# New prices for scans, row sums, transpositions and scaled additions in the engine model that orders a mixer layer's work

## The chip, the cores and the metric

One core of one Trainium2 chip runs the whole layer. The metric is the device time of one execution in microseconds (us), the median of several runs. The engines are TensorE (PE, matrix products, with its weight loads shown as PEld), VectorE (DVE), ScalarE (ACT), GpSimd (POOL) and SyncE (SP, which here only starts transfers). Each works through a list of its own in order, and they wait for each other by semaphores.

## The reference: what is computed

A layer on 256 tokens of width 2048, in float32: a SwiGLU block, a token mixer, a second SwiGLU block, each added to its input, and a last norm.

```python
x = x + 0.5 * swiglu(rms_norm(x, ffn1_norm), w_gate, w_up, w_down)      # inner width 5632
proj = rms_norm(x, mix_norm) @ w_in
y = concat(rwkv7_mix(proj[..., :3360]), hgrn2_mix(proj[..., 3360:]))    # 16 heads x 64, 8 heads x 128
x = x + y @ w_out
x = x + 0.5 * swiglu(rms_norm(x, ffn2_norm), w_gate2, w_up2, w_down2)
return rms_norm(x, final_norm)
```

The mixer has two recurrences over the tokens. `rwkv7_mix` is a delta rule with a decay for each channel; `hgrn2_mix` is a gated linear recurrence. Both are computed here in blocks of tokens.

## The kernel before

**Weights.** Nearly all of PE's time goes into products with weights. They come from memory in pieces of 128x1024 float32 (`raw`), one after the other in the order of the list `pieces`. To keep float32's accuracy, a piece is split in two: ACT rounds it to a shorter form (`hi<-raw`), and DVE or POOL subtracts that from the piece (`lo<-raw,hi`). PE multiplies with hi on all 256 tokens in two levels (512 columns) and with lo on the upper level alone (256 columns), so a piece is 8 + 8 matmuls. There are four buffers for raw, hi and lo each. When piece i is used up, `split_to(i + 5)` puts the split of a later piece on ACT's and DVE's or POOL's lists, about three pieces ahead of its use. In the first eight pieces and the last four lo always goes to DVE. In the others `spare` chooses: it goes to POOL if the model says that DVE would be done with it over 1500 ns later than POOL while mixer work is pending, or later at all while none is.

**The mixer's work.** The mixer's products with weights (jobs k, r, v for rwkv, and f, q, i, g for hgrn, in two halves 0 and 1 of the heads) stand in one loop (`for i, kk, part in order()`). Everything else of the mixer runs beside them, in generators: `rwkv(half)` and `hgrn(half)`. After every matmul of the loop `poll` gives the first two pending generators a step if `max(V.until, S.until)`, the model's time at which DVE's and ACT's lists are done, is at most 2500 ns behind the model's time of PE. Inside a generator `need(tile)` puts the rest off until the model says that the tile is ready.

**The model.** V, S and G wrap the three engines (class `Engine`). Each call of an operation goes through `call` in `__getattr__`: it asks `cost` for the operation's time, a fixed part and a rate for each element of a partition, moves the engine's `until` on by it and notes in `model.ready` when the output will be there. `Products` does the same for PE, whose time `model.pe` is the model's now. No number of the model reaches the chip; it only decides in which order instructions are written and which engine takes a lo. A scheduler then keeps that order by and large when it fills each engine's list.

**Names in the mixer.** In the rwkv half, k's section scales with `tensor_scalar` on POOL, takes reciprocals and `scalar_tensor_tensor` products on DVE, 128x256 at a time and four for a half, then 128x1024 products on POOL (`t<-t,t`) and DVE, then running products over tokens (`tensor_tensor_scan`, 128x260, four for each call, which the order of the program prints as SCALAR_TENSOR_TENSOR b8<-b8,cst), and products into the operands `b8`. Then follows a chain of 62 dependent small products on DVE, for which `state["chain"]` is set, so that lo stays on DVE. The hgrn half works in levels s = 0 to 7: for each DVE makes a product `t<-t,tot` and POOL one `q<-q,tot`, and PE multiplies the two (`ps<-q,t`).

Of the kernel before, what the change touches and what calls it, by code (L numbers as in the profile page):

```python
# [97 lines left out]
def names_of(xs):  # L98
    return [getattr(getattr(x, "tensor", x), "name", None) for x in xs if hasattr(x, "shape")]
# [21 lines left out]
class Engine:  # L121
# [3 lines left out]
    def cost(self, op, n):  # L125
        rate = self.model.RATE[self.name]
        if op == "reciprocal":
            rate *= 6
        elif self.name == "vector" and op in ("tensor_copy", "tensor_scalar"):
            rate *= 0.6  # L130
        elif self.name == "gpsimd" and op == "memset":
            rate *= 0.2
        elif op == "dma_start":
            return 1000.0
        return self.model.FIXED[self.name] + rate * n
# [4 lines left out]
    def __getattr__(self, op):  # L140
        fn = getattr(self.engine, op)

        def call(*args, **kwargs):
            m = self.model
            cost = self.cost(op, math.prod(args[0].shape[1:]))
            begin = max(self.until, m.now())
            self.until = begin + cost
            done = max(begin, m.wait(*args)) + cost + m.LATENCY + (5000.0 if op == "dma_start" else 0.0)
            for n in names_of(args[:1]):
                m.ready[n] = done  # L150
            return fn(*args, **kwargs)  # L151

        return call
# [1217 lines left out]
```

## Time and profile before

| | |
|---|---|
| time, median of 3 runs | 2063.84 us (2062.35 to 2064.65) |
| the profiled execution | 2062.84 us, of which the span is 2061.1 |
| PE busy | 2017.2 us, 98% of the span |
| DVE busy | 1377.9 us, 67% |
| ACT busy | 1006.0 us, 49% |
| POOL busy | 390.2 us, 19% |
| mean granted clock of PE | 0.99 of full speed |
| lo's made by DVE (128x1024) | 605, mean 1350 ns |
| lo's made by POOL (128x1024) | 70, mean 2617 ns |

The profile counts an engine as busy from the start to the end of its instructions. A matmul's end is modelled, so the place to look at is where PE does not have a next matmul to start. An idle time in the timelines stands in brackets with what ended it: [3.65 <-POOL lo L151] means that the engine stood still for 3.65 us until POOL's lo was there. L151 is the line of the helper through which every operation of DVE, ACT and POOL goes, and L171 and L175 are those of PE. Buffer numbers are left out of the names in the trace.

### The profile page before, as it was taken

How to read it: one execution, taken by the hardware profiler on the slowest of the kernel's cores; microseconds unless marked ns; L12 is line 12 of the kernel's file. 1: busy time of each engine (PE TensorE's matmuls, PEld its weight loads, DVE VectorE, ACT ScalarE, POOL GpSimd, SP SyncE). 2: the span in 40 equal slices, each digit the busy share in tenths (PEclk: the TensorE clock that was granted, in tenths of full speed). 3: DMA queues.
4: the chain of work that ended last, by engine and by line, in shares of the span. 5: the costliest groups of instructions: out<-in, count | busy, mean ns of one | idle time of the engine just before them, and what ended most of it. 6: DMA issues, size and time to landing. Idle time of an engine off the chain costs nothing.

```text
span 2061.1 us, 31577 instructions
## 1 busy us (share of the span) xinstructions
PE 2017.2 (98%) x12766; PEld 1762.0 (85%) x12766; DVE 1377.9 (67%) x1498; ACT 1006.0 (49%) x1199; POOL 390.2 (19%) x220
## 2 busy tenths in 40 slices
PE   8999999999999999899989899999999999999998
PEld 7888888888888888788868788888888888888887
DVE  7665565555565688986888668856565655555657
ACT  6444444444444466465556545544444344434434
POOL 1221110111011032322343104222111011101101
PEclk9999999999999999999999999999999999999999
DMA  7655665556556565443434435555656555655653
GB/s 252 202 183 191 194 191 187 188 185 194 190 184 194 185 233 174 155 138 124 131 115 149 150 105 182 190 189 183 194 187 191 189 187 189 195 191 184 194 187 120
DMA packets 106146, 368.33 MB, mean 179 GB/s; under 512 B 11632, under 2 KB 18032, under 8 KB 105744
## 3 DMA queue, kind: packets, MB, share of 16 engines
q1 hardware_dynamic: 104352, 359.97, 54.0%
q0 software_dynamic: 1104, 6.06, 0.8%
q8 instruction: 100, 1.64, 0.3%
q14 instruction: 46, 0.38, 0.1%
q10 hardware_dynamic: 544, 0.28, 0.0%
HBM read 362.08 MB, written 4.19 MB: 178 GB/s over the span
## 4 chain that ended last, share of the span: by engine, by line
PE 50%; DVE 2%; POOL 1%; issue 0%; ACT 0%; DVEq 0%; POOLq 0%; ACTq 0%
PE mm L171 46%; PE ps L171 4%; DVE t L151 1%; POOL t L151 1%; DVE lo L151 1%; ACT t L151 0%; DVE xts L151 0%; DVE b L151 0%; POOL lo L151 0%; PE ps L175 0%; POOL b L151 0%; ACT hi L151 0%; DVEq L1367 0%; ACT inv L151 0%; ACT itok L151 0%
## 5 line engine op out<-in xcount | busy, mean ns | idle before, releaser
L171 PE MATMUL mm<-t,hi 128*128 128x512 f32 x5264 | 1287.0, 393 | 4.8 <-DVE t L151 4.3
L171 PEld LDWEIGHTS mm<-t,hi 128*128 128x128 f32 x5264 | 961.6, 189 | 189.1 <-ACT hi L151 3.9
L151 DVE TENSOR_TENSOR lo<-raw,hi 128x1024 fp32r<-128x1024 f32 (+1 forms) x615 | 818.6, 1335 | 403.2 <-ACT hi L151 379.7
L151 ACT CAST hi<-raw 128x1024 fp32r<-128x1024 f32 (+1 forms) x685 | 712.8, 1042 | 685.1 <-PE mm L171 426.9
L171 PEld LDWEIGHTS mm<-t,lo 128*128 128x128 f32 x5296 | 695.3, 191 | 52.8 <-POOL lo L151 11.4
L171 PE MATMUL mm<-t,lo 128*128 128x256 f32 x5296 | 712.0, 284 | 13.8 <-POOL lo L151 10.5
L151 POOL TENSOR_TENSOR lo<-raw,hi 128x1024 fp32r<-128x1024 f32 x70 | 183.2, 2617 | 548.3 <-ACT hi L151 529.7
L151 POOL TENSOR_TENSOR t<-t,inv 128x1024 f32<-128x1024 f32 x22 | 69.0, 3134 | 730.2 <-ACT t L151 730.2
L151 DVE TENSOR_TENSOR t<-mm,t 128x512 f32<-128x512 f32 x122 | 83.7, 686 | 171.1 <-ACT t L151 171.1
L151 ACT COPY t<-mm 128x512 f32<-128x512 f32 x122 | 71.4, 585 | 241.2 <-PE mm L171 225.9
L151 DVE TENSOR_TENSOR t<-t,t 128x512 fp32r<-128x512 f32 (+25 forms) x243 | 124.5, 516 | 13.9 <-ACT t L151 7.6
L151 DVE SCALAR_TENSOR_TENSOR xts<-mm,xts 128x512 f32<-128x512 f32 x126 | 86.6, 687 | 28.0 <-PE mm L171 27.6
L151 ACT CAST t<-t 128x512 fp32r<-128x512 f32 x72 | 43.7, 616 | 13.1 <-DVE t L151 4.9
L151 DVE TENSOR_TENSOR t<-t,inv 128x1024 f32<-128x1024 f32 (+1 forms) x35 | 42.5, 1215 | 1.0
L151 DVE RECIPROCAL t<-t 128x256 f32<-128x256 f32 x24 | 41.4, 1736 | 2.4 <-ACT t L151 2.3
L151 POOL TENSOR_TENSOR t<-t,t 128x1024 f32<-128x1024 f32 (+1 forms) x9 | 25.4, 2820 | 73.3 <-ACT hi L151 45.0
L151 DVE SCALAR_TENSOR_TENSOR t<-xts,vec,t 128x256 fp32r<-128x256 f32 x48 | 28.6, 616 | 12.5 <-ACT t L151 12.4
L151 ACT ACTIVATE t<-t 128x1024 f32<-128x1024 f32 (+2 forms) x32 | 32.7, 1023 | 4.5 <-DVE t L151 4.4
L151 ACT COPY t<-ps 32x512 f32<-32x512 f32 (+8 forms) x44 | 19.7, 448 | 27.4 <-PE ps L171 26.4
L151 ACT ACTIVATE t<-xts,vec 128x256 fp32r<-128x256 f32 x48 | 23.0, 504 | 19.5 <-DVE xts L151 18.3
L171 PE MATMUL mm<-hi,t 128*128 128x512 f32 x128 | 32.4, 392 | 0.0
L151 POOL TENSOR_TENSOR t<-t 128x1020 f32<-128x1020 f32 (+1 forms) x7 | 17.5, 2506 | 65.9 <-DVE t L151 48.0
(134 smaller groups left out, 723.0 us busy)
## 6 DMA issues: line engine op xcount, KB each, us to landing
raw<-in_ffn_w_up_dram SPq DMA_DIRECT2D x176, 512.0 KB, 3.9
raw<-in_ffn_w_down_dram SPq DMA_DIRECT2D x176, 512.0 KB, 3.4
raw<-in_ffn_w_gate_dram SPq DMA_DIRECT2D x173, 512.0 KB, 3.9
raw<-in_w_in_dram SPq DMA_DIRECT2D x96, 512.0 KB, 3.3
raw<-in_w_out_dram SPq DMA_DIRECT2D x32, 512.0 KB, 3.3
raw<-in_w_i_dram SPq DMA_DIRECT2D x16, 512.0 KB, 3.3
raw<-in_w_lora_dram SPq DMA_DIRECT2D x6, 512.0 KB, 3.4
spill<-xts POOLq DMA_DIRECT2D x1, 2048.0 KB, 10.8
```

The lines of the kernel that those rows point to most:

```text
L151: return fn(*args, **kwargs)
L171: return self.engine.matmul(out, a, b, **kwargs)
```

## The change

The method that prices an operation gets three more cases: a row sum or a scan counts twice the rate, a transposition on DVE 1.5 times, a `scalar_tensor_tensor` on DVE of up to 256 elements 1.8 times. And a row sum is counted by the elements that it reads (`args[1]`) and no longer by those that it writes. The rest of the file is the same; its lines are numbered 6 higher.

```diff
@@ -126,6 +126,12 @@
         rate = self.model.RATE[self.name]
         if op == "reciprocal":
             rate *= 6
+        elif op in ("tensor_reduce", "tensor_tensor_scan"):
+            rate *= 2
+        elif self.name == "vector" and op == "transpose":
+            rate *= 1.5
+        elif self.name == "vector" and op == "scalar_tensor_tensor" and n <= 256:
+            rate *= 1.8
         elif self.name == "vector" and op in ("tensor_copy", "tensor_scalar"):
             rate *= 0.6
         elif self.name == "gpsimd" and op == "memset":
@@ -142,7 +148,7 @@
 
         def call(*args, **kwargs):
             m = self.model
-            cost = self.cost(op, math.prod(args[0].shape[1:]))
+            cost = self.cost(op, math.prod(args[op == "tensor_reduce"].shape[1:]))
             begin = max(self.until, m.now())
             self.until = begin + cost
             done = max(begin, m.wait(*args)) + cost + m.LATENCY + (5000.0 if op == "dma_start" else 0.0)
```

By DVE's fixed 90 ns and 1.04 ns for an element the model's prices go from 356 to 569 ns for a 128x256 `scalar_tensor_tensor`, from 360 to 631 for a scan of 260, from 356 to 2220 for a row sum of 128x1024 to 128x256, from 1155 to 1687 for a 128x1024 transposition.

All engines together do the same operations as before, but for one more load of an activation table on ACT, and 14 lo's (128x1024) are made by POOL that DVE made before: one at the start, five at the end of the first FFN, three more between the mixer's start and the end of the second rwkv half's k section, five behind that. Many operations of DVE, ACT and POOL change places in the mixer. The three places below are those that the prediction speaks of.

The first is POOL's list in the k section of the first rwkv half: scalings t<-t,vec of 128x256, products t<-t,t of 128x1024, and lo's. Before:

```order
L151 TENSOR_SCALAR t4_6876<-t4_6877,vec_92 128x256
L151 TENSOR_TENSOR lo_7142<-raw_7034,hi_7141 128x1024
L151 TENSOR_SCALAR t4_6876<-t4_6877,vec_92 128x256 x2
L151 TENSOR_TENSOR t4_6877<-t4_6877,t4_7074 128x1024
L151 TENSOR_SCALAR t4_6876<-t4_6840,vec_92 128x256 x4
L151 TENSOR_TENSOR t4_6876<-t4_6876,t4_7082 128x1024
L151 TENSOR_TENSOR lo_7195<-raw_7114,hi_7194 128x1024
L151 TENSOR_TENSOR b8_7396<-t4_7082,b8_7235 128x16x64
```

After:

```order
L157 TENSOR_SCALAR t4_6890<-t4_6891,vec_92 128x256 x3
L157 TENSOR_TENSOR lo_7192<-raw_7090,hi_7191 128x1024
L157 TENSOR_SCALAR t4_6890<-t4_6891,vec_92 128x256
L157 TENSOR_TENSOR t4_6891<-t4_6891,t4_7124 128x1024
L157 TENSOR_SCALAR t4_6890<-t4_6840,vec_92 128x256 x4
L157 TENSOR_TENSOR t4_6890<-t4_6890,t4_7058 128x1024
L157 TENSOR_TENSOR b8_7424<-t4_7058,b8_7253 128x16x64
L157 TENSOR_TENSOR t4_7296<-t4_7186 128x4x255
L157 TENSOR_TENSOR lo_7407<-raw_7327,hi_7406 128x1024
```

No lo stands right behind both 128x1024 products any more, where lo_7195 did; one (lo_7192) stands ahead of them, between the third and the fourth scaling, and the next (lo_7407) behind the whole section.

The second is POOL's list at the same section of the second rwkv half. Before:

```order
L151 TENSOR_TENSOR t4_8998<-t4_8998,t4_9235 128x1024
L151 TENSOR_SCALAR t4_8997<-t4_8677,vec_92 128x256 x4
L151 TENSOR_TENSOR t4_8997<-t4_8997,t4_9065 128x1024
L151 TENSOR_TENSOR lo_9354<-raw_9245,hi_9353 128x1024
L151 TENSOR_TENSOR t4_9320<-t4_9167 128x4x255
L151 TENSOR_TENSOR b8_9604<-t4_9065,b8_9440 128x16x64
```

After:

```order
L157 TENSOR_TENSOR t4_9268<-t4_9155 128x4x255
L157 TENSOR_SCALAR t4_9127<-t4_9128,vec_92 128x256 x4
L157 TENSOR_TENSOR t4_9128<-t4_9128,t4_9359 128x1024
L157 TENSOR_SCALAR t4_9127<-t4_8604,vec_92 128x256 x4
L157 TENSOR_TENSOR lo_9423<-raw_9299,hi_9422 128x1024
L157 TENSOR_TENSOR t4_9127<-t4_9127,t4_9031 128x1024
L157 TENSOR_TENSOR b8_9650<-t4_9031,b8_9488 128x16x64
L157 TENSOR_TENSOR lo_9535<-raw_9446,hi_9534 128x1024
```

The lo in the group (lo_9354 before, lo_9423 after, of other weights) now stands ahead of the second 128x1024 product, the product t<-t of 128x4x255 has gone from behind the group to ahead of it, and one more lo (lo_9535) stands behind the product into b8.

The third is DVE's list at the chain of 62 small products (t2) of the second rwkv half, into which lo's and the levels' products t4<-t4,tot are mixed. Before, its end:

```order
L151 TENSOR_TENSOR t2_9946<-t2_9946,t2_9947 128x2x15
L151 TENSOR_TENSOR lo_10297<-raw_10168,hi_10296 128x1024
L151 TENSOR_TENSOR t2_9947<-t4_9944,t2_9946 128x16
L151 TENSOR_TENSOR t4_10223<-t4_10122,tot0_10124 128x64x8
L151 TENSOR_TENSOR t2_9946<-t2_9946,t2_9947 128x16
L151 TENSOR_TENSOR t4_10344<-t4_10223,tot1_10225 128x32x16
```

After, its beginning:

```order
L157 STREAM_TRANSPOSE t4_10084<-t4_10029 128x1024
L157 TENSOR_TENSOR lo_10108<-raw_9900,hi_10107 128x1024
L157 TENSOR_TENSOR t2_10087<-t4_10084,t2_10086 128x31
L157 TENSOR_TENSOR t4_10175<-t4_10073,tot0_10075 128x64x8
L157 TENSOR_TENSOR t2_10086<-t2_10086,t2_10087 128x31
```

And after, its end:

```order
L157 TENSOR_TENSOR t2_10086<-t2_10086,t2_10087 128x2x15
L157 TENSOR_TENSOR t2_10087<-t4_10084,t2_10086 128x16
L157 TENSOR_TENSOR t4_10302<-t4_10175,tot1_10177 128x32x16
L157 TENSOR_TENSOR lo_10475<-raw_10362,hi_10474 128x1024
L157 TENSOR_TENSOR t4_10355<-mm_10201,t4_10355 128x512
L157 TENSOR_TENSOR t2_10086<-t2_10086,t2_10087 128x16
```

The 64x8 product moves from the chain's end to right behind its first link, and the next level's, 32x16, takes the place at the end.

## Rows read from the trace of the kernel before

**Rows 1.** Table by stage: stretch and length, each engine's busy us, clock, DMA.

```profile
core 0: us, PE busy (x) PEld busy (x) DVE busy (x) ACT busy (x) POOL busy (x), PEclk, DMA share, GB/s
42.00:820.00 778.00, 778.00 (x4475) 686.67 (x4474) 492.34 (x471) 367.29 (x409) 125.28 (x51) 1.00 0.59 192
820.00:1275.00 455.00, 426.18 (x3610) 358.19 (x3609) 364.95 (x496) 256.37 (x349) 139.26 (x108) 0.98 0.42 136
1275.00:2048.00 773.00, 773.00 (x4474) 684.09 (x4473) 481.67 (x474) 351.73 (x390) 115.64 (x42) 1.00 0.58 185
...
800.00:850.00 50.00, 46.26 (x259) 39.70 (x258) 48.42 (x43) 31.18 (x37) 24.07 (x14) 0.97 0.40 130
```

**Rows 2.** PE's timeline: start, us, what, count, in brackets idle before and releaser.

```profile
838.12 2.08 PE L171 MATMUL mm<-t,lo 128*128 128x256 f32 x8 [3.65 <-POOL lo L151]
...
861.78 1.10 PE L171 MATMUL ps<-t,bones_r 128*128 128x512 f32 x3 [0.74 <-DVE t L151]
...
1048.00 1.21 PE L171 MATMUL mm<-t,lo 128*128 128x256 f32 x8 [1.38 <-DVE lo L151]
...
1057.91 2.07 PE L171 MATMUL mm<-t,lo 128*128 128x256 f32 x8 [6.86 <-POOL lo L151]
...
1069.98 1.21 PE L171 MATMUL mm<-t,lo 128*128 128x256 f32 x8 [1.02 <-DVE lo L151]
...
1145.00 1.08 PE L171 MATMUL ps<-q,t 128*32 128x32 f32 x64 [6.80 <-DVE t L151]
```

**Rows 3.** The table by stage again, right behind each long wait.

```profile
838.00:841.30 3.30, 3.17 (x12) 2.89 (x13) 3.30 (x2) 0.00 (x0) 3.22 (x2) 0.50 0.44 159
...
1058.00:1063.20 5.20, 5.20 (x17) 4.43 (x18) 1.31 (x4) 0.00 (x0) 3.85 (x2) 0.50 0.59 202
...
1145.00:1148.50 3.50, 3.50 (x72) 3.15 (x73) 3.50 (x5) 2.33 (x6) 3.34 (x6) 0.50 0.46 149
```

**Rows 4.** POOL's timeline at the first rwkv half's k section.

```profile
825.68 3.44 POOL L151 TENSOR_TENSOR t<-t,t 128x1024 f32<-128x1024 f32 x1
...
835.34 2.73 POOL L151 TENSOR_TENSOR lo<-raw,hi 128x1024 fp32r<-128x1024 f32 x1
```

**Rows 5.** DVE's timeline at the same place.

```profile
825.63 1.22 DVE L151 SCALAR_TENSOR_TENSOR t<-t,t 128x1024 f32<-128x1024 f32 x1 [0.84 <-POOL t L151]
826.77 3.43 DVE L151 TENSOR_TENSOR lo<-raw,hi 128x1024 fp32r<-128x1024 f32 x1
...
830.73 5.21 DVE L151 TENSOR_TENSOR_SCAN b<-b,cst 128x260 f32<-128x260 f32 x4
835.97 3.18 DVE L151 SCALAR_TENSOR_TENSOR b<-t,b 128x1024 f32<-128x1024 f32 x1
...
843.44 2.46 DVE L151 TENSOR_TENSOR_SCAN b<-b,cst 128x260 f32<-128x260 f32 x4
```

**Rows 6.** POOL's timeline at the second rwkv half's k section.

```profile
1042.85 0.48 POOL L151 TENSOR_SCALAR t<-t,vec 128x256 f32<-128x256 f32 x1 [1.65 <-DVE t L151]
1043.42 3.44 POOL L151 TENSOR_TENSOR t<-t,t 128x1024 f32<-128x1024 f32 x1
1046.86 5.04 POOL L151 TENSOR_SCALAR t<-t,vec 128x256 f32<-128x256 f32 x4
...
1054.54 3.31 POOL L151 TENSOR_TENSOR lo<-raw,hi 128x1024 fp32r<-128x1024 f32 x1
```

**Rows 7.** DVE's timeline at the second rwkv half's chain of small products.

```profile
1113.42 0.21 DVE L151 TENSOR_TENSOR t<-t,t 128x31 f32<-128x31 f32 x1
...
1119.87 1.21 DVE L151 TENSOR_TENSOR lo<-raw,hi 128x1024 fp32r<-128x1024 f32 x1
...
1144.16 0.69 DVE L151 TENSOR_TENSOR t<-t,tot 128x512 f32<-128x512 f32 x1
```

**Rows 8.** Timelines of POOL and DVE near the first FFN's end.

```profile
709.95 2.41 POOL L151 TENSOR_TENSOR lo<-raw,hi 128x1024 fp32r<-128x1024 f32 x1 [69.28 <-ACT hi L151]
...
710.81 1.83 DVE L151 SCALAR_TENSOR_TENSOR t<-xts,vec,t 128x256 fp32r<-128x256 f32 x1 [0.58 <-ACT t L151]
...
713.70 0.47 DVE L151 SCALAR_TENSOR_TENSOR t<-xts,vec,t 128x256 fp32r<-128x256 f32 x1
```

## The prediction, made before the changed kernel ran

> **What bounds the kernel now.** I read four views in this order. First the table by stage: outside the mixer TensorE (PE) never stands still, 778.00 of 778 us in the stretch from 42 to 820 us and 773.00 of 773 after 1275 us, and between 820 and 1275 us it is busy 426.18 of 455 us [rows 1]. So all that a new order can win lies in those 455 us: 455 − 426.18 = 28.8 us of standing still. Work cannot be won anywhere else, since the change alters no PE instruction. Second, PE's own timeline of the mixer, for where the 28.8 us stand. Three places hold most of it. Place A: 3.65 us for a lo that POOL makes, then small waits, of which one of 0.74 us is shown and two more of 0.54 and 0.56 us lie beside it. Place B: 1.38, 6.86 and 1.02 us for lo's, the longest again for one made on POOL. Place C: 6.80 us for a product that DVE makes [rows 2]. Together 21.5 us; the other 7.3 us are a dozen waits of 0.2 to 1.5 us. Third, the granted clock: in the stretch right behind the beginning of each long wait it is 0.50, that is the 1.2 GHz level, and PE works 3.17, 5.20 and 3.50 us at it [rows 3]. At half speed half of that is lost: 1.6, 2.6 and 1.8 us, 6.0 in all. The ceiling of any reordering is therefore 28.8 + 6.0 = 34.8 us, 1.7% of the time. Fourth, the timelines of POOL and DVE at the three places, which show what stood ahead of the late tile.
>
> **Place A (first rwkv half, around 820 to 866 us).** Before, POOL takes a 128x1024 product of 3.44 us at 825.68, four scalings and a second product, and only then the lo (lo_7195), at 835.34, which ends at 838.07; PE starts at 838.12 [rows 2, 4]. PE wanted it at 838.12 − 3.65 = 834.47. After, the one lo on POOL at this place (lo_7192) stands ahead of that group, between the third and the fourth scaling, and the second lo of POOL (lo_7407) stands behind the whole group. POOL is at that point of its list at about 825.7 us, when the group begins [rows 4]; a lo takes 2.73 us there [rows 4], and even with 3 us of being held up it is done by 831.4. The long wait goes, with its half clock: −3.65 − 1.6 = −5.25. What is late next: the fourth scaling now waits for that lo, and DVE's product of k (1.22 us at 825.63, after 0.84 us of waiting for POOL [rows 5]) waits for the scaling, so it begins 2.7 to 6.4 us later, at 828.3 to 832.0. Behind it DVE has three lo's (3.43 us for one beside a POOL product, 1.2 for the other two), the four scans (2.46 us without POOL beside them, 5.21 with it), the product into b (3.18 us beside POOL, 1.2 at the least, as the k product of the same size) and lo_7303 (1.2 to 3.43), with 1.1 us for the k product and 0.6 for one more [rows 5]. The sum runs from 12.4 to 19.4 us, so lo_7303 is there between 840.7 and 851.4. PE wants it four pieces of weights after 834.47. A piece is 16 matmuls, by the stretch without a wait 778.00 / 4475 x 16 = 2.78 us [rows 1], so at 845.6. The new wait is 0 to 5.8 us; I take the middle, 2.9, and with it half of the old clock loss, 0.8. A: −5.25 + 2.9 + 0.8 = about −1.6, between −5.3 and +2.1.
>
> **Place B (second rwkv half, around 1040 to 1070 us).** Before, POOL's group of product, four scalings, product, lo begins at 1043.42 and its lo ends at 1054.54 + 3.31 = 1057.85: 14.4 us [rows 6]. PE wanted it at 1057.91 − 6.86 = 1051.05 [rows 2], so the group began 7.6 us ahead of the need. After, the second product stands behind the lo. It takes 1054.54 − (1046.86 + 5.04) = 2.6 us, so the group down to the lo is 11.8 us; and since the scans that ran on DVE beside the scalings come later now, the 5.04 us of scalings may shrink, down to 4 x 0.48 = 1.9 us by the one that stands alone at 1042.85 [rows 6]: 8.7 to 11.8. But the group also begins later against the need. In the order of the program 69 matmuls stand between the first product and the first use of the lo before, 54 after; 15 matmuls at 2.78 us for 16 are 2.6 us. So the group has 5.0 us, and the wait is 3.7 to 6.8; I take 5.2. The two waits beside it, 1.38 and 1.02 us, I put at half, 1.2 together, since neither lo keeps its neighbours, and the clock at 2.2. B: (5.2 + 1.2 + 2.2) − (9.26 + 2.6) = −3.3, between −6 and +1.
>
> **Place C (chain of 62 small DVE products beside the hgrn levels, 1107 to 1150 us).** Before, DVE's chain begins at 1113.42 and the product that PE waits for begins at 1144.16, behind 61 of the 62 links, nine lo's of 1.21 us and three other kinds [rows 7]. After, the 64x8 product stands behind the chain's first link and the next one, 32x16, takes the place at its end: one product less of 0.69 us, or 0.6 from start to start, on DVE; one lo and one predicated copy stand ahead of the chain instead of in it, which leaves the end where it was. PE has 1.0 us more of matmuls between the last score product and the waiting one (32.0 against 30.9 us, each at the pace that the trace shows). So the wait is 6.80 − 0.6 − 1.0 = 5.2, and half of the clock loss behind it that hangs on its length, 0.4, goes too. C: −2.0, between −4 and +1.
>
> **The rest.** Of the 14 lo's that go from DVE to POOL, one lies at the start and five at the end of the first FFN, where PE does not stand still with eight of them on POOL already [rows 1]; they cost nothing; the cover is DVE's slack there, and without it each could cost the 1.4 us worked out next. Three more than before lie between 820 and 1060 us of the mixer, the others behind it. What a lo on POOL does to DVE is in the trace: from 709.95 to 712.36 POOL makes one, and DVE's 128x256 product that begins at 710.81 takes 1.83 us, against 0.47 for the same product a little later [rows 8]. So a moved lo saves DVE its 1.2 us and can cost it 1.4. For three of them up to 4.1 us on DVE, where it is busy 48.42 of 50 us [rows 1]; a third of it, 1.3, reaches PE by my choice, since only stretch A is that full. The first chain starts some 5 us of matmuls later against the hgrn levels beside it, whose waits are among the small ones; I put 0.5 us for that. The earlier row sums at the start and one more activation table on ACT (busy 256 of 455 us [rows 1]) I put at nothing; bounds ±1. The rest: +1.8, between −4 and +5 (the small waits are 7.3 us in all, and one more wait like that of A would be 5).
>
> The Trainium skill, "SBUF — State Buffer", section "Who interferes with whom", says that a DVE instruction with two inputs in SBUF and a GpSimd instruction that reads SBUF exclude each other for the whole instruction, so that the second waits until the first is done. The trace agrees here: the stretched product ends at 712.64, 0.28 us behind POOL's lo. If by that rule the whole 4.1 us reached PE, the rest would be +4.6 and the sum −2.3 instead of −5.1.
>
> **Sum.** −1.6 − 3.3 − 2.0 + 1.8 = −5.1 us. The profiled execution took 2062.84 us (span 2061.1 and 1.7 around it), so its like would take 2057.7. The median of the runs is 1.0 us above it, 2063.84, and against that the forecast is 2058.7 us.
>
> **Rivals.**
> 1. The waits only change place. For it: DVE is full at A [rows 1], no work is taken away, and A's new wait and B's old one are ranges that reach to what is there now. The new prices also stay wrong where the trace has the widest spread: a scan is 0.6 us alone and 1.3 beside POOL [rows 5], and one price cannot be both. Against it: the lo's at A and B do stand nearer the head of POOL's list. Time: 2063.8, give or take 3. The Trainium skill, "Perfetto Trace Analysis", section "Optimizing Scalar/DVE Operations", warns that moving work between GpSimd and DVE may not help because they share a read port; by that rule this is the outcome, and the stretched product [rows 8] speaks for it.
> 2. Slower, by one mechanism: at B a second lo (lo_9535) stands on POOL behind the product into b, which waits for the scans that DVE now makes later, behind three lo's. If DVE is as late there as it was before, that lo comes as late as the first. A second wait like the old one costs 6.86 + 2.6 = 9.5 us; the sum becomes +4.4, 2068.2. It decides for slower from a loss of 5.1 us on. Against it: between the place where it is queued and its first use PE has 9.0 us of matmuls.
> 3. Both waits for POOL go almost wholly: A at its lower end (−5.3), B without the scans beside the scalings (−6), C at −4, and the rest at +1: −14.3, 2049.5. For it speaks that the scans, which stretch POOL's scalings, no longer run beside them at B; against it that DVE must still feed all three places.
>
> **How the numbers follow.** Forecast (gain of 2 to 9 us): 0.45. Rival 1: 0.25. Rival 2: 0.20. Rival 3: 0.10. A measurement of this kernel can tell about 0.2%, 4.1 us, from no change. Faster by more than that: 0.7 of the forecast, all of rival 3, a tenth of rival 1: 0.44. Slower by more: nearly all of rival 2 and a seventh of rival 1: 0.23. Within it: 0.33. The range runs from rival 3's time to rival 2's, 2050 to 2068.
>
> **What would show it.** Right at A: no wait of over 3 us for POOL around 834 us, and a smaller one, for DVE's lo, some four pieces later. Right at B: one wait of 4 to 7 us for a POOL lo, and no second one behind it; a second one is rival 2. Right at C: a wait of about 5 us for DVE's product, at the end of the chain. If the mixer's stretch loses as much as before, 28 us, with the waits elsewhere, rival 1 is it. Wrong altogether would be a wait outside the 455 us, or a changed number of PE's instructions.

## The result, and the profile after

The changed kernel takes 2083.67 us (median, 2082.48 to 2085.62) against 2063.71 of the kernel before on the same chip: a ratio of 1.0098, 95% interval 1.0087 to 1.0110. It is 20 us slower. The forecast was 2058.7, and the range ended at 2068.

The table by stage of the changed kernel (columns as in [rows 1]), its profiled execution having a span of 2083.8 us:

```profile
0.00:42.00 42.00, 35.16 (x177) 29.32 (x178) 31.80 (x44) 26.95 (x43) 8.24 (x15) 0.96 0.78 266
42.00:820.00 778.00, 777.21 (x4465) 685.58 (x4465) 486.81 (x462) 362.30 (x401) 133.42 (x55) 1.00 0.59 192
820.00:1275.00 455.00, 424.60 (x3567) 357.96 (x3564) 355.98 (x479) 257.70 (x353) 145.43 (x111) 0.96 0.40 133
1275.00:1345.00 70.00, 60.84 (x337) 52.20 (x336) 56.17 (x63) 32.30 (x43) 32.66 (x14) 0.95 0.45 153
1345.00:2048.00 703.00, 703.00 (x4043) 621.21 (x4042) 422.36 (x389) 311.15 (x332) 98.77 (x35) 1.00 0.59 189
```

Two of these stretches in the kernel before:

```profile
0.00:42.00 42.00, 36.32 (x186) 29.77 (x187) 33.29 (x46) 27.85 (x44) 5.46 (x14) 1.00 0.80 274
1275.00:1345.00 70.00, 70.00 (x406) 61.85 (x405) 56.82 (x62) 40.76 (x50) 19.24 (x8) 1.00 0.58 188
```

The two long stretches of plain weights are as they were but for 0.8 us at the end of the first FFN. Between 820 and 1275 us PE now stands still for 30.4 us instead of 28.8, and a new stretch loses as well: 9.2 us between 1275 and 1345 us, where the mixer ends and the second FFN starts and where nothing was lost before. The clock of the two stretches is 0.96 and 0.95. The start loses 1.2 us more than before.

Where the waits are, by PE's timeline (columns as in [rows 2]). First the places that the prediction named, A (859 to 874 us), B (1076 to 1103) and C (1167):

```profile
859.01 1.22 PE L177 MATMUL mm<-t,lo 128*128 128x256 f32 x8 [1.55 <-DVE lo L157]
868.70 0.50 PE L177 MATMUL ps<-t,bones_r 128*128 128x512 f32 x1 [1.70 <-DVE t L157]
873.44 0.66 PE L181 MATMUL ps<-cst,b 128*128 128x128 f32 x4 [1.52 <-DVE t L157]
...
1076.10 1.22 PE L177 MATMUL mm<-t,lo 128*128 128x256 f32 x8 [0.64 <-POOL lo L157]
1088.50 1.21 PE L177 MATMUL mm<-t,lo 128*128 128x256 f32 x8 [0.96 <-POOL lo L157]
...
1102.60 1.30 PE L177 MATMUL mm<-t,lo 128*128 128x256 f32 x8 [2.07 <-POOL lo L157]
...
1167.23 1.34 PE L177 MATMUL ps<-q,t 128*32 128x32 f32 x32 [4.91 <-DVE t L157]
```

(At B there is one more, of 0.34 us for a lo of DVE.) Then the waits that were not there, or were under 1 us, in the kernel before:

```profile
946.16 0.24 PE L177 MATMUL ps<-t,t 32*32 32x32 f32 x2 [2.37 <-ACT t L157]
...
1027.10 0.50 PE L177 MATMUL ps<-t,bones_r 128*128 128x512 f32 x1 [2.62 <-ACT t L157]
1031.02 1.65 PE L177 MATMUL ps<-t,bones_r 128*128 128x512 f32 x3 [3.42 <-DVE t L157]
...
1056.90 3.68 PE L177 MATMUL ps<-t,t 64*128 64x256 f32 x14 [3.64 <-DVE t L157]
...
1180.68 1.12 PE L177 MATMUL ps<-q,t 128*64 128x64 f32 x16 [2.03 <-DVE t L157]
...
1291.24 2.08 PE L177 MATMUL mm<-t,hi 128*128 128x512 f32 x4 [6.78 <-DVE t L157]
...
1337.97 2.08 PE L177 MATMUL mm<-t,hi 128*128 128x512 f32 x8 [1.43 <-DVE xts L157]
```

At A, B and C the kernel did what was forecast, or better: 3.65 us for POOL's lo became 1.55 for DVE's, 6.86 became at most 2.07, 6.80 became 4.91 [rows 2]. But the second list has 22 us that the prediction does not know of. And each wait of over 2 us has work at half clock behind it. The stretches of the changed kernel at 0.50, by the table by stage:

```profile
35.30:38.60 3.30, 3.30 (x12) 2.75 (x11) 3.30 (x4) 0.63 (x2) 0.00 (x0) 0.50 0.93 328
...
946.60:953.40 6.80, 6.64 (x87) 6.07 (x88) 3.75 (x4) 5.74 (x14) 1.88 (x3) 0.50 0.52 168
1028.60:1035.30 6.70, 4.28 (x12) 3.60 (x13) 6.70 (x6) 1.44 (x2) 1.82 (x1) 0.50 0.36 129
1055.90:1062.60 6.70, 5.70 (x22) 4.95 (x23) 5.14 (x10) 4.76 (x10) 0.00 (x0) 0.50 0.24 78
1103.70:1107.00 3.30, 3.30 (x10) 2.62 (x9) 2.21 (x2) 0.00 (x0) 0.00 (x0) 0.50 0.93 284
1165.10:1171.80 6.70, 4.57 (x43) 4.15 (x44) 5.93 (x12) 3.48 (x8) 2.35 (x3) 0.50 0.47 159
1182.20:1185.50 3.30, 3.30 (x15) 3.02 (x14) 0.96 (x4) 1.68 (x5) 1.52 (x4) 0.50 0.60 179
1288.00:1294.70 6.70, 3.46 (x9) 2.79 (x10) 4.97 (x8) 2.18 (x3) 0.00 (x1) 0.50 0.23 78
```

Eight stretches instead of three [rows 3], the first of them at the start. PE works 34.6 us in them, so by half of it 17.3 us are lost, against 5.9 before. The balance: the two profiled spans differ by 22.7 us. The standing still grows by 12.8 us of it (1.6 and 9.2 in the two stretches above, 0.8 at the end of the first FFN, 1.2 at the start). The other 9.9 us are PE's busy time, 2027.1 us after 2017.2, for the same matmuls: that is the clock, for which halving gives 11.4, a little too much.

### The profile page after: what moved, and what is told of

Its sections match the earlier page's. It is cut to its first block, busy times and chain, and to the rows that moved or that the text cites. A ratio compares the mean times of both kernels' runs of the same rounds, so it can differ in the third digit from the quotient of the medians.

```text
span 2083.8 us, 31591 instructions
## 1 busy us (share of the span) xinstructions
PE 2027.1 (97%) x12766; PEld 1770.8 (85%) x12766; DVE 1378.0 (66%) x1484; ACT 1005.2 (48%) x1200; POOL 425.5 (20%) x234
## 5 line engine op out<-in xcount | busy, mean ns | idle before, releaser
L177 PE MATMUL mm<-t,hi 128*128 128x512 f32 x5264 | 1291.1, 393 | 15.2 <-DVE t L157 10.4
L157 DVE TENSOR_TENSOR lo<-raw,hi 128x1024 fp32r<-128x1024 f32 (+1 forms) x601 | 805.3, 1345 | 401.5 <-ACT hi L157 379.6
L157 POOL TENSOR_TENSOR lo<-raw,hi 128x1024 fp32r<-128x1024 f32 x84 | 222.6, 2653 | 554.6 <-ACT hi L157 554.6
L157 DVE SCALAR_TENSOR_TENSOR t<-xts,vec,t 128x256 fp32r<-128x256 f32 x48 | 40.3, 858 | 18.5 <-ACT t L157 18.4
L157 DVE TENSOR_TENSOR t<-t,inv 128x1024 f32<-128x1024 f32 (+1 forms) x35 | 46.9, 1339 | 0.9
L177 PE MATMUL ps<-t,t 32*32 32x32 f32 (+5 forms) x352 | 29.8, 273 | 6.4 <-DVE t L157 3.6
L157 ACT ACTIVATE t<-t 128x1024 f32<-128x1024 f32 (+2 forms) x32 | 32.8, 1024 | 5.5 <-DVE t L157 5.5
L177 PEld LDWEIGHTS ps<-t,t 32*32 32x32 f32 (+4 forms) x352 | 24.7, 154 | 11.2 <-DVE t L157 3.8
```

The source lines that it names most:

```text
L177: return self.engine.matmul(out, a, b, **kwargs)
```

## The experiments

A position in the program's order is given as in the expectations, in us of matmuls: the sum over PE's matmuls that are written ahead of the instruction, each at the pace that the trace shows. It says how late the program puts something against PE's work, and nothing of how long anything waits. Three theories stood against each other. **Late**: higher prices make the gate hold the mixer's steps back, so they come late against the matmuls that need them. **POOL**: the 14 lo's that moved to POOL block DVE. **Scatter**: the order before was by chance a good one, and any other loses.

### Each price alone

The edits are the four parts of the change, one at a time. An experiment is named below by the first part of its label (e1, e2, ...). Scans, then scaled additions:

```diff
+        elif op == "tensor_tensor_scan":
+            rate *= 2
```

```diff
+        elif self.name == "vector" and op == "scalar_tensor_tensor" and n <= 256:
+            rate *= 1.8
```

> Only the new price of scans (twice the rate); row sums, transpositions and scaled additions keep the old one. Two lo's move to POOL; the second chain of small products begins 11 us of matmuls later in the program's order than before, the last reciprocals of the second rwkv half 6 us later. Theory 'late' (a higher price makes the model hold the mixer's steps back, so they come late against the matmuls that need them): +10 to +16 us against the kernel before, with the wait at the start of the output projection in it. Theory 'POOL' (the lo's that moved to POOL block DVE): +2 to +3 us, two of fourteen lo's. Theory 'scatter' (any new order loses or wins by chance): anywhere from -10 to +20.

Measured: 2080.74 us, ratio 1.0080 (1.0065 to 1.0095), +17 us: a little above what 'late' gave, and far above 'POOL'.

> Only the new price of scaled additions (1.8 times the rate up to 256 elements). Four lo's move to POOL; the second chain begins 5 us of matmuls later than before, the last reciprocals at the same place as before. Theory 'late': +3 to +8 us, and none of it at the start of the output projection. Theory 'POOL': +5 to +6. Theory 'scatter': -10 to +20.

Measured: 2074.98 us, ratio 1.0058 (1.0041 to 1.0075), +11 us: more than 'late' or 'POOL' gave. Its tail is hardly late (1.1 and 1.2 us at the output projection); its waits are 4.41 us near 863, 2.61 and 3.43 near 1028 and 3.64 near 1056 us, the last three as in the changed kernel.

Row sums, then transpositions:

```diff
+        elif op == "tensor_reduce":
+            rate *= 2
...
-            cost = self.cost(op, math.prod(args[0].shape[1:]))
+            cost = self.cost(op, math.prod(args[op == "tensor_reduce"].shape[1:]))
```

```diff
+        elif self.name == "vector" and op == "transpose":
+            rate *= 1.5
```

> Only the new price of row sums (twice the rate, counted by the elements read). Seven lo's move to POOL, five of them at the end of the first FFN; the mixer's own steps stand where they stood, none is later. Theory 'late': 0 to +3 us, from the norms' small waits at the start and around the second norm. Theory 'POOL': +8 to +10, half of the fourteen lo's. Theory 'scatter': near 0 too, since nearly nothing in the mixer moves.

Measured: 2065.20 us, ratio 1.0007 (0.9998 to 1.0017). Half of the moved lo's come with 1.4 us, which is not clear of no change.

> Only the new price of transpositions on DVE (1.5 times the rate). No lo moves to POOL; both chains begin where they began, the k section of the second rwkv half lies 2 to 6 us of matmuls later in parts. Theory 'late': -1 to +4 us. Theory 'POOL': 0. Theory 'scatter': -10 to +20.

Measured: 2066.70 us, ratio 1.0015 (1.0005 to 1.0024), +3 us.

The loss comes from two of the four prices, scans and scaled additions, and the four do not add up: 17 + 11 + 1.4 + 3 = 32 us against 20. The number of lo's on POOL is out as the main cause: seven come with 1.4 us, two with 17. The seven are no test of a single place in the mixer, though: five of them lie at the end of the first FFN.

### The gate alone

`BEHIND` is the lead that the gate grants; only this number is changed. The first two have the old prices, and BEHIND 2000 (below) and 3000; the next two have the new prices, and 3000 and 4000.

```diff
-BEHIND = 2500.0
+BEHIND = 2000.0
```

> The old prices, BEHIND 2000: the mixer's steps are held back without any price being changed. The chains begin at 868.8 and 1063.4 us of matmuls, the last reciprocals 13 us later than before; 68 lo's are on POOL, two fewer than before. Theory 'late': +15 to +25 us against the kernel before, with a wait at the start of the output projection. Theory 'scatter': -5 to +20. Theory 'POOL': 0 or less.

Measured: 2085.45 us, ratio 1.0109 (1.0094 to 1.0124), +22 us, with no price changed and fewer lo's on POOL. Holding the steps back is enough to make a loss of this size.

> The old prices, BEHIND 3000: the mixer's steps go out earlier than before (chains at 861.6 and 1043.8 us of matmuls, the last reciprocals 15 us earlier). Theory 'late': -6 to +2 us. Theory 'scatter': -5 to +20.

Measured: 2078.08 us, ratio 1.0074 (1.0057 to 1.0091), +15 us. 'Late' misses here: earlier steps cost too. The longest wait is the one at C, which was 6.80 us:

```profile
1149.86 1.98 PE L171 MATMUL ps<-q,t 128*32 128x32 f32 x128 [9.45 <-DVE t L151]
```

> All new prices, but the gate that holds mixer steps back opens 500 ns earlier (BEHIND 3000 instead of 2500). In the program's order both chains then begin where they began in the kernel before (at 865.4 and 1042.6 us of matmuls instead of 870.0 and 1054.0) and the last reciprocals of the second rwkv half 14 us earlier than with the new prices alone; 88 lo's are on POOL, four more than with the new prices. Theory 'late': most of the loss comes back, 2063 to 2069 us, and the wait of over 6 us at the start of the output projection goes. Theory 'scatter' (an order that fits the old prices was found, and any other loses): still 2070 to 2090. Theory 'POOL': 2084 or more, since more lo's are on POOL.

Measured: 2071.27 us, ratio 1.0044 (1.0029 to 1.0058). With the chains back at their old places 12 us of the 20 come back, less than 'late' expected; the wait at the output projection is 0.9 us again. What is left is mostly one wait for a lo on POOL at A, longer than the 3.65 us of the kernel before:

```profile
848.21 2.08 PE L177 MATMUL mm<-t,lo 128*128 128x256 f32 x8 [8.13 <-POOL lo L157]
```

> All new prices, BEHIND 4000. The chains begin at 861.6 and 1046.5 us of matmuls, the last reciprocals 14 us earlier than with the new prices alone. Theory 'late': 2058 to 2069 us. Theory 'scatter': 2070 to 2090.

Measured: 2089.47 us, ratio 1.0129 (1.0114 to 1.0144), the slowest of all, with 7.6 us and 5.9 us for POOL's lo's and 10.4 for DVE's product at C. 'Late' misses here by 20 us.

So with the old prices a lead of 2500 ns is better than 2000 and than 3000; with the new ones 3000 is better than 2500 and than 4000. Too short a lead makes PE wait for the mixer's products (10.95 us at C and 10.82 at the output projection with BEHIND 2000). Too long a lead also loses, but not in one way: with the new prices PE waits longer for lo's of POOL, with the old ones at C.

### Without lo's on POOL in the mixer

```diff
-        return V if state["chain"] or late <= (1500.0 if bg else 0) else G
+        return V if state["chain"] or late <= (1e9 if bg else 0) else G
```

> The old prices, but no lo goes to POOL while mixer work is pending (62 on POOL instead of 70, none in the mixer), so that DVE's list in the model is longer. Both chains begin later, at 872.8 and 1063.7 us of matmuls (865.4 and 1042.9 before), the last reciprocals 15 us later. Theory 'late': +15 to +25 us, with a wait at the start of the output projection. Theory 'POOL' (a lo on POOL is what hurts): -5 to -15 us, since the two waits for POOL's lo's, 10.5 us and their half clock, cannot occur.

Measured: 2080.23 us, ratio 1.0084 (1.0069 to 1.0099), +17 us. 'POOL' had expected a gain. The lo's fill DVE's list in the model, the gate holds the steps back, and the tail is late again. The waits at the start of the output projection in the two kernels with old prices and held-back steps, the one of BEHIND 2000 and this one:

```profile
1294.64 3.78 PE L171 MATMUL mm<-t,hi 128*128 128x512 f32 x8 [10.82 <-DVE t L151]
```

```profile
1288.75 3.78 PE L171 MATMUL mm<-t,hi 128*128 128x512 f32 x8 [10.79 <-DVE t L151]
```

In the kernel before that wait is short:

```profile
1271.44 1.17 PE L171 MATMUL mm<-t,hi 128*128 128x512 f32 x4 [0.93 <-DVE t L151]
```

Over all kernels it follows the place of the second rwkv half's last reciprocal in the program:

| kernel | last reciprocal, us of matmuls | wait at the output projection, us |
|---|---|---|
| earlier steps or new prices in one half (e5, e6, e8, e9, e11) | 1138 to 1152 | 0 to 0.9 |
| both cures (e18, below) | 1151.3 | 1.7 |
| scaled additions alone; first half (e12, e13, e14) | 1152.5; 1153.0 | 1.1 + 1.2; 0.5 + 1.2 |
| before; row sums; half the addition (e16); transpositions | 1153.9; 1153.9; 1153.9; 1154.1 | 0.93; 0.92; 0.93; 0.77 |
| scans alone | 1159.7 | 6.1 |
| changed kernel; sections apart (e17) | 1160.9; 1160.9 | 6.78; 6.81 |
| all new, MARGIN 1000 | 1163.2 | 7.05 |
| old prices, BEHIND 2000 | 1166.7 | 10.82 |
| old prices, no lo on POOL | 1169.4 | 10.79 |

Up to 1154 the wait is 0 to 2.3 us, and behind that it grows by 0.6 to 0.9 us for each us. This part of the loss is shown: it is being late, and scans' price does it.

### The halves, and an earlier gate in the second

The new prices hold only while the gate's clock (it counts steps of the weight loop) is under 640, that is up to the last steps of the first half of the heads, or only from there on:

```diff
-        elif op in ("tensor_reduce", "tensor_tensor_scan"):
+        elif self.model.new() and op in ("tensor_reduce", "tensor_tensor_scan"):
...
+    def new(self):
+        return self.clock[0] < 640
```

> The new prices up to the last steps of the first half of the heads, the old ones from there on. The first chain begins at 870.0 (865.4 before), the second at 1047.9 us of matmuls (1042.9 before), its k section 14 us later than before, the last reciprocals at the same place as before. Theory 'late': +5 to +12 us, from the steps between the two chains, and no wait over 2 us at the start of the output projection. Theory 'scatter': -10 to +20.

Measured: 2062.48 us, ratio 1.0001 (0.9991 to 1.0010). No loss, where 'late' gave 5 to 12.

> The old prices up to the last steps of the first half of the heads, the new ones from there on. The second chain begins at 1046.0 us of matmuls (1042.9 before), the last reciprocals at 1150, 4 us earlier than before; eight more lo's are on POOL than before, all from the second half on. Theory 'late': -4 to +4 us. Theory 'POOL': +8 to +12. Theory 'scatter': -10 to +20.

Measured: 2065.49 us, ratio 1.0012 (1.0002 to 1.0021), +2 us, with eight more lo's on POOL than before. Each half costs next to nothing; only both together lose. The second chain begins at 1042.9 in the kernel before, at 1047.9 in the one, at 1046.0 in the other and at 1054.0 with both: the lateness adds up over the halves.

The next has all new prices, and a wider gate from the second half on:

```diff
-            if task[1] <= clock[0] and max(V.until, S.until) <= model.now() + BEHIND:
+            if task[1] <= clock[0] and max(V.until, S.until) <= model.now() + (BEHIND if clock[0] < 640 else 3500.0):
```

> All new prices, BEHIND 2500 through the first half of the heads and 3500 from its last steps on, so that the second chain begins at 1042.9 us of matmuls, where it began in the kernel before (1054.0 with the new prices alone), and the last reciprocals at 1152, as before (1161). The first half is that of the changed kernel to the instruction. Theory 'late': the wait of 6.8 us at the start of the output projection and the one behind it go, with their stretch of half clock; 2068 to 2076 us. Theory 'scatter': that wait is no different from the others and another takes its place; 2078 to 2090.

Measured: 2079.59 us, ratio 1.0080 (1.0063 to 1.0097). The wait at the output projection went, as 'late' had it, but the time is above what it gave. The waits near 1028 and 1053 us stay, 5.07 and 3.79 us where the changed kernel has 2.62 + 3.42 and 3.64, and new ones come behind them: 1.88 and 4.11 us near 1100, and 6.79 at C where the changed kernel has 4.91. So there is a second cause, between the two chains.

### The second cause: two sections beside each other

The next two kernels have the new prices up to clock 640 and up to clock 680, with row sums at the old price in both. Of e14 against e13:

```diff
-        return self.clock[0] < 640
+        return self.clock[0] < 680
```

> As the kernel with the new prices in the first half of the heads alone, but row sums at the old price. In the mixer it differs from that kernel by nothing but lo's on POOL; the order of the start of the first norm is that of the kernel before. All theories: 0 to -3 us against that kernel, that is 2059 to 2064 us; it is the base for the next run.

Measured: 2062.54 us, ratio 0.9996 (0.9986 to 1.0005).

> As the run before it, but the new prices stay some 55 us of matmuls longer, through the y section of the first half and into the k section of the second. The chains begin where they begin there (870.0 and 1047.9), the last reciprocals stand at the same 1153; but the k section's first reciprocal stands at 978.0 us of matmuls, behind two of the y section's, as in the changed kernel, and not at 986.0. Theory 'crowded' (two sections on DVE at once, with PE's matmuls for them queued): waits of 2 to 4 us for bones_r and for ps<-t,t 64x256 appear between 1020 and 1056 us as in the changed kernel, +7 to +13 us against the run before it. Theory 'late' alone: 0 to +2. Theory 'scatter': -10 to +10.

Measured: 2067.78 us, ratio 1.0032 (1.0021 to 1.0042): 5 us above the run before it, less than the 7 to 13 that 'crowded' gave. The two waits for bones_r near 1024 and 1028 us, which e13 does not have, are those of the changed kernel to a hundredth; the third one, 3.64 us there and 2.60 in e13, is 0.73 + 1.39 here:

```profile
1024.20 0.49 PE L181 MATMUL ps<-t,bones_r 128*128 128x512 f32 x1 [2.61 <-ACT t L161]
1028.13 1.65 PE L181 MATMUL ps<-t,bones_r 128*128 128x512 f32 x3 [3.43 <-DVE t L161]
1048.31 1.13 PE L181 MATMUL ps<-t,t 64*128 64x256 f32 x4 [0.73 <-DVE t L161]
1051.73 1.46 PE L181 MATMUL ps<-t,t 64*128 64x256 f32 x8 [1.39 <-DVE t L161]
```

The bones_r matmuls add up k's squares over a head. ACT makes the squares and rounds them, DVE subtracts to get what the rounding left off, and PE needs both parts. In the order of e13 the matmuls are written 8.5 us of matmuls behind DVE's two subtractions; in that of e14 0.7 us behind them, since the model says that their inputs are ready. On the chip they are not. The order of e14 has two more lo's on POOL than that of e13, and both are made here (1010.21 and 1015.90). The timelines of DVE, ACT and POOL in e14 (start, us, what, idle before):

```profile
1010.54 3.43 DVE L161 TENSOR_TENSOR t<-t,inv 128x1024 f32<-128x1024 f32 x1
...
1015.97 3.78 DVE L161 SCALAR_TENSOR_TENSOR t<-t,vec,t 128x256 f32<-128x256 f32 x4 [1.80 <-POOL t L161]
...
1019.85 0.51 ACT L161 ACTIVATE t<-t,vec 128x256 f32<-128x256 f32 x1 [6.92 <-DVE t L161]
...
1025.37 3.30 DVE L161 TENSOR_TENSOR t<-t,t 128x512 fp32r<-128x512 f32 x2
```

```profile
1010.21 2.67 POOL L161 TENSOR_TENSOR lo<-raw,hi 128x1024 fp32r<-128x1024 f32 x1 [2.28 <-ACT hi L161]
1014.05 1.89 POOL L161 TENSOR_TENSOR t<-t 128x1020 f32<-128x1020 f32 x1 [1.17 <-DVE t L161]
1015.90 2.38 POOL L161 TENSOR_TENSOR lo<-raw,hi 128x1024 fp32r<-128x1024 f32 x1
...
1025.18 2.34 POOL L161 TENSOR_TENSOR lo<-raw,hi 128x1024 fp32r<-128x1024 f32 x1 [3.28 <-ACT hi L161]
```

Three steps on the way to these matmuls run on DVE beside a lo of POOL: the scaling of k (a product), the four scaled additions behind it, for which ACT's first square waits 6.92 us, and the two subtractions. In e13 POOL has no lo there before 1020 us, and DVE's rows are shorter:

```profile
1010.36 1.23 DVE L161 TENSOR_TENSOR t<-t,inv 128x1024 f32<-128x1024 f32 x1
...
1012.68 1.29 DVE L161 TENSOR_TENSOR t<-t,t 128x512 fp32r<-128x512 f32 x2
...
1019.24 1.27 DVE L161 SCALAR_TENSOR_TENSOR t<-t,vec,t 128x256 f32<-128x256 f32 x3
...
1020.71 2.42 POOL L161 TENSOR_TENSOR lo<-raw,hi 128x1024 fp32r<-128x1024 f32 x1 [4.53 <-ACT hi L161]
...
1022.10 2.18 DVE L161 TENSOR_TENSOR t<-t,t 128x512 fp32r<-128x512 f32 x2
...
1031.27 1.09 PE L181 MATMUL ps<-t,bones_r 128*128 128x512 f32 x4
```

The product takes 3.43 us against 1.23, the four additions 3.78 against 1.7 (by the three in 1.27), the subtractions 3.30 against 1.29 for two of the kind without POOL beside them (1012.68). That is 6.3 us more, an estimate, and the two waits are 6.0 in sum. In e13 the subtractions are held up as well, 2.18 us at 1022.10, but their matmuls come 7 us later and do not wait.

So moved lo's do have a part here, at the one place where matmuls stand right behind what they delay. e14 changes the lo's and the order at once, and no run separates the two.

All new prices, and a step that waits for its operands with no margin of its own is written 1000 ns of the model behind their end:

```diff
-MARGIN = 0.0
+MARGIN = 1000.0
```

> All new prices, and a step that waits for a tile is let go 1000 ns later (MARGIN 1000 instead of 0), so that PE's mixer matmuls stand further behind their inputs. The chains begin where they begin with the new prices (870.0, 1054.0), the last reciprocals 1 to 2 us later. If the waits between the chains come from matmuls queued too close behind their inputs: they shrink by 1 us each, 2076 to 2081 us. Theory 'late': 2084 to 2088.

Measured: 2087.03 us, ratio 1.0115 (1.0100 to 1.0130). The two waits for bones_r became 2.46 and 1.58 us, 2 us less in sum, as expected; but the next one grew from 3.64 to 5.78, and the tail became later still, so the time came out where 'late' had it. More distance by delay is no cure.

The price of scaled additions alone (e2), at half the addition:

```diff
-            rate *= 1.8
+            rate *= 1.4
```

> Only the price of scaled additions is new, at half the addition (1.4 times the rate instead of 1.8). Both chains begin where they began in the kernel before, the last reciprocals too; the k sections shift by 1 to 4 us of matmuls. If the loss follows the dose: half of the 11 us of the full price, +5. Theory 'crowded': the sections keep apart (first k reciprocal at 976, the last of the y section at 969.5), so -2 to +3. Theory 'scatter': -10 to +15.

Measured: 2064.47 us, ratio 1.0005 (0.9996 to 1.0015). At half the addition nothing is lost, where the full one loses 11: the loss does not follow the dose. That the sections keep apart in this order, as 'crowded' had it, fits; it is not tested by itself.

### Both causes taken away in the changed kernel

The old prices stand from clock 640 to 699, the new ones everywhere else; then the same with the earlier gate behind that stretch.

```diff
-        return self.clock[0] < 640
+        return not 640 <= self.clock[0] < 700
```

```diff
-            if task[1] <= clock[0] and max(V.until, S.until) <= model.now() + BEHIND:
+            if task[1] <= clock[0] and max(V.until, S.until) <= model.now() + (BEHIND if clock[0] < 700 else 3500.0):
```

> The new prices everywhere but for the 60 steps of the gate's clock around the first half's y section, where the old ones stand. The k section of the second half then begins behind the y section (first reciprocal at 986.0 us of matmuls instead of 978.0), while the chains (870.0, 1054.0) and the last reciprocals (1160.9) stand as in the changed kernel; 81 lo's on POOL instead of 84. Theory 'crowded and late': the waits of 2.6 and 3.4 us near 1024 to 1031 go with their half clock, the one of 6.8 at the output projection stays: 2075 to 2080 us. If the loss is only of being late: 2082 to 2085. Theory 'scatter': 2065 to 2090, with the waits elsewhere.

Measured: 2075.26 us, ratio 1.0057 (1.0042 to 1.0072), 8.4 us below the changed kernel. The waits for bones_r between 1020 and 1036 us are gone, the one at the output projection is untouched:

```profile
1280.93 2.07 PE L181 MATMUL mm<-t,hi 128*128 128x512 f32 x4 [6.81 <-DVE t L161]
```

> As the run before it, and from the end of that stretch on the gate opens 1000 ns earlier (BEHIND 3500): the second chain begins at 1047.2 and the last reciprocals stand at 1151.3 us of matmuls (1153.9 in the kernel before). Theory 'crowded and late': the wait of 6.8 us at the output projection goes too, with its half clock: 2066 to 2072 us. Theory 'scatter': 2065 to 2090 with a large wait elsewhere.

Measured: 2065.19 us, ratio 1.0010 (1.0000 to 1.0020), another 10 us below. The wait at the output projection:

```profile
1269.71 2.11 PE L181 MATMUL mm<-t,hi 128*128 128x512 f32 x8 [1.68 <-DVE t L161]
```

The two edits together take away 18.5 of the 20 us: being late at the tail, and the order beside the first half's y section. They shorten waits that neither theory named as well (the part on the prediction says which). What stays is within 2 us of the kernel before. No kernel of these beats that one by more than can be measured. 'Scatter' in its strong form is out: e12, e13 and e16 have other orders than the kernel before and lose nothing that can be measured, and the two edits, aimed at the two causes, came out within 1 us of the ranges given for them.

## Why the prediction was wrong

**What bounds the kernel**: right. The mixer was the place (its tail now lies behind 1275 us), PE's instructions did not change, and the clock behind each wait had to be counted. But the ceiling was worked out for a gain alone. The loss had no bound but the sum of rival 2, +4.4 us, and it came out at 20.

**Place A**: the long wait for POOL's lo went, as forecast, but the wait that was worked out in its place did not come. lo_7303 ended at 848.8 us, inside the forecast 840.7 to 851.4, and PE came to it at that moment, 3 us later than taken, and waited 0.02 us. The 1.55 us at 859 are for a lo of DVE three pieces later, which the working does not have, and the waits for bones_r and for b behind it grew from 0.74 and 0.56 to 1.70 and 1.52 us; no half clock. In sum 4.8 us against 5.5 + 1.6: −2.3, forecast −1.6. That the sums are close is luck.

**Place B**: the direction was right, the size was not. Waits of 0.64, 0.96, 0.34 and 2.07 us, 4.0 in all, and 1.7 of clock, against 9.3 + 2.6: −6.2, forecast −3.3. POOL's list shows why the first of them, for the lo in the group, is 0.64 us and not 5.2:

```profile
1066.49 3.44 POOL L157 TENSOR_TENSOR t<-t,t 128x1024 f32<-128x1024 f32 x1
1069.93 3.76 POOL L157 TENSOR_SCALAR t<-t,vec 128x256 f32<-128x256 f32 x4
1073.66 2.39 POOL L157 TENSOR_TENSOR lo<-raw,hi 128x1024 fp32r<-128x1024 f32 x1
```

The group takes 9.6 us, inside the forecast 8.7 to 11.8, since the scalings shrank from 5.04 to 3.76 us. But it begins 9.0 us ahead of the need (1075.46 us), not 5.0. The 54 matmuls between them are 9.4 us. The forecast took it that POOL would come to the group as late against the order as before, where 69 matmuls, 12.0 us, had become 7.6.

**Place C**: right to the tile. 4.91 us for the 32x16 product at the chain's end, forecast 5.2, with the clock loss 2.3 after 1.8 before: −1.4, forecast −2.0.

So the three places gave −9.9 us, more than the −6.9 that was forecast for them. **The rest** is the step that failed: forecast +1.8 between −4 and +5, it is about +30 by the medians (+33 by the two profiled executions). The failing was in how it was made. It was bounded by the waits that the trace of before shows there (7.3 us of small ones), while a new order can make waits at places where the old one had none, up to the slack that is used up there. Of the signs for it the prediction has one, the first chain later by 5 us of matmuls, priced at 0.5 us. The second chain's start at 1054.0 against 1042.9, and the last reciprocal at 1160.9 against 1153.9, stood in the order of the program and were not carried to the end of the mixer, where the next matmul (the output projection) needs them. That is 5.9 us of waiting and half of 3.46 us of clock. The k section's first reciprocal close behind the y section's last one (1.6 us of matmuls, 5.2 before) stood there too, and with it the matmuls for k's squares: 6.0 us of waiting and half of about 4.3 us of clock. Together these two are some 16 us. The other new waits, near 946, 1057, 1181 and after 1299 us, are 9.5 us, and with half of the 15.6 us of work at half clock behind them 17, as much as the two that are explained. Of these the runs show no cause, only that e17 and e18 have smaller ones in the first two places (1.9 and 2.6 us). And the start, which the prediction put at nothing, has 1.2 us more of standing still and 1.7 of clock in the profiled execution.

**The rivals**: the slower one was given 0.20, with a mechanism that did not occur. It expected a second long wait for POOL's lo at B; the two there are 0.96 and 2.07 us. Rival 1's sign came for its stretch, 30.4 us of standing still in the 455 with the waits elsewhere, but not its time: it had neither the clock nor the tail. The sign for being wrong altogether came too, a wait outside the 455 us (1291). The case that came, the tail too late for the output projection, was not among the rivals, though its price could be had: a wait of up to the 7 us by which the last reciprocal is later.

**Contention**: the rule of the Trainium skill, "SBUF — State Buffer", section "Who interferes with whom", that a DVE operation with two inputs in SBUF and one of POOL that reads SBUF exclude each other, holds in e14, where the trace agrees (3.43 us beside POOL's lo against 1.23). In the kernel before it is as plain: 44 of the 46 lo's of DVE that overlap with one of POOL end 1.08 us behind POOL's, almost their whole 1.22 us. The outcome that the Trainium skill, "Perfetto Trace Analysis", section "Optimizing Scalar/DVE Operations", suggests, no help from work moved between the two, is what row sums alone and the second half alone show: +1.4 and +2 us with seven and eight lo's moved. Neither page would have given the 20 us.

## What to carry to other kernels

When a planner's prices change, look first at where its order puts the last step of each stage against the matmul that needs it, and only then at the waits of the old trace: lateness adds up over stages, costs nothing while there is slack and then, here, 0.6 to 0.9 us of waiting for each us. A gate that was tuned with the old prices is part of them: with the new ones a lead of 3000 ns loses 8 us where 2500 loses 20. A price nearer to a measured duration is no improvement by itself: the scan's new price, 631 ns, is what the scans take undisturbed (2.46 us for four [rows 5]), and it alone cost 17 us.

## What was not expected of the hardware

Waits of PE much shorter than the three of the kernel before are followed by work at half clock. In the changed kernel a wait of 2.37 us ends at 946.16, and the granted clock from 946.6 to 953.4 us is 0.50, that is 1.2 GHz; PE's 6.64 us of work in that stretch lose more than the wait itself. A wait of 2.03 us before 1180.68 is followed by 3.30 us of work at 0.50, while none follows the one of 1.55 us before 859.01. The length of a wait alone does not tell: in e17 the clock is 0.50 from 868.1 to 871.3 us behind a wait of 1.57 us that ends at 867.52, and in the changed kernel it does not fall behind one of 1.70 us that ends at 868.70. Nor does the program: e17 and e18 are the same up to the second half of the heads and have the same wait of 1.91 us near 34 us, but the clock of the first 42 us is 0.96 in e17 and 1.00 in e18. More and shorter waits in place of a few long ones were therefore no gain here: of the changed kernel's loss against the kernel before, 9.9 us are clock.
